# Convolved blocks turned by VectorE and DRAM instead of TensorE, with a longer weight rotation at the pooled blocks

## The chip, the core and the metric

The kernel runs on one core of a Trainium2 chip. The metric is the device time of one execution in microseconds (us). A core has five engines that run their own instruction streams and wait for each other by semaphores: TensorE (PE in the profile; its weight loads are PEld), VectorE (DVE), ScalarE (ACT), GpSimd (POOL) and SyncE (SP), which here only issues transfers. ScalarE and GpSimd issue transfers too. The profile shows issuing in the queue rows (SPq, ACTq). On-chip memory has 128 partitions; a tile is a rectangle of partitions and bytes in it.

## The reference

One layer of a diffusion backbone in float32: 512 latent tokens and 256 context tokens of width 1024. After a modulated RMSNorm, one projection (1024 columns in, 4640 out) feeds three groups of heads. What matters here is the beginning of that:

```
p = u @ w_in                                # u: normalised, modulated tokens
z, xbc, dt, pool, q, k, v = split(p)        # widths 1024, 1536, 32, 512, 512, 512, 512
xbc = silu(dwconv(xbc, conv_w, conv_b))     # 3 taps along the tokens, per channel
xs, B, C = split(xbc)                       # 1024, 256, 256 channels
pooled = [mean over w neighbours - pool  for w in (2, 4, 8, 16)]   # 128 channels each
y = pooled @ w_pool * pool_scale
```

xs, B and C go into a state space scan in both directions (SSD), k and v with q into a neighbourhood attention. The modulation vectors are `silu(c) @ ada_w + ada_b`, with a matrix of 1024 x 6144; two of its six parts are needed only at the second half of the layer. Behind all this come the output projection, another normalisation, and a feed-forward part that picks 16 of 16,384 experts for each of 8 heads (PEER).

## The kernel before, in words

**Three matmuls for one.** Float32 products are made from split operands: `h` is the rounded high part, `l` the remainder, and `mm3` adds h·h, h·l and l·h (L220 to L222, and L460 to L466 where latent and context tokens share the weights). For that, each weight block is loaded to a tile `wraw` by SP (L241), ScalarE makes `wh` from it (L210), VectorE makes `wl` (L213).

**The weight stream.** `Stream` (L224 to L250) keeps a list of raw tiles and a list of split pairs and goes around both in turn: load number i takes raw tile i modulo the length of the list. Through the stage of interest there are three raw tiles ("G") and two split pairs, and `ws.keep(3, 2)` ahead of it sets the counters to 0. `extend` adds tiles to a list, `keep` cuts the lists and resets the counters.

**The stage around the change** (54 to 217 us of the span), on TensorE:

1. Twelve blocks of 128 channels of xbc, the loop `for cb in range(12)` (L664). Blocks 0 to 7 are xs, 8 and 9 B, 10 and 11 C. `projT` (L522) loads a weight block and makes the block transposed: channels on partitions, 512 latent tokens in one PSUM bank and, for blocks under 10, 256 context tokens in another. ScalarE copies both into `xp` (L669, L672), VectorE makes the three taps in `c1` (L675 to L677), ScalarE the silu (L683, for C blocks L679). Since xs and B are needed with tokens on partitions too, TensorE turns each of the ten blocks in six transposes of 128x128 (L687 four, L693 two) into PSUM; VectorE copies four back (L688) and ScalarE two (L694), into `xsn` (six tiles of 128 tokens by 1024 channels) or `Bn`. The tiles of this loop, `xp`, `c1`, `sT` and others, are in the pool `tmpC` on the right side of memory, closed at L698.
2. Four pooled blocks, b = 3 to 0 (L737 on). Each has two `projT`: PL (the pooled channels) and K (keys). GpSimd sums the windows (`pool_sums`, L711), VectorE subtracts (`pool_diff`), TensorE multiplies by w_pool (`pool_out`). The pool `plp` of this stage, with `pl`, `pa`, `pb`, lies on the right side as well, where `tmpC` was.
3. Decays and V0: `decays` (L756) and four loads of `projC`. Then `plp` is closed, and the SSD stage begins; it reads `xsn` first at L902.

Beside this, the modulation sums run on VectorE: `ada_sum(bank, k)` (L551) multiplies two pieces of ada_w, 128 x 1024 each, by a scalar per partition and adds them up in `adac`. SP loads each piece into one of the input tiles that are free by then, `xin` = three parts of kT, qT0, qT1, vc; from the tenth step on into the last three of them in turn (L558). One step of this generator `ada` is taken in blocks cb >= 3 and twice per pooled block; the sums keep their program order on VectorE.

**What sets the order.** The streams of each engine are put in order by the scheduler of the language from the code's dependences; those marked `keep_in_program_order` keep the order of the code. Tiles of a closed pool give their memory to the pool opened next; an instruction that writes such memory waits until the former readers and writers are done.

Of the kernel before, what the change touches and what calls it, by code (L numbers as in the profile page):

```python
# [7 lines left out]
F32 = mybir.dt.float32  # L8
# [4 lines left out]
AF = mybir.ActivationFunctionType  # L13
ALU = mybir.AluOpType
# [143 lines left out]
def build(tc, A, out, dbg=None):  # L158
    nc = tc.nc
    V, S, G, PE = nc.vector, nc.scalar, nc.gpsimd, nc.tensor  # L160
    dbg = dbg or {}

    def dump(name, ap):
        if name in dbg:
            nc.sync.dma_start(dbg[name], ap)
# [53 lines left out]
    def mm3(ps, ah, al, bh, bl, start, stop):  # L219
        PE.matmul(ps, ah, bh, start=start, stop=False)  # L220
        PE.matmul(ps, ah, bl, start=False, stop=False)  # L221
        PE.matmul(ps, al, bh, start=False, stop=stop)  # L222
# [29 lines left out]
    def kpc(src):  # L252
        return src.rearrange("(k p) c -> p k c", p=P)
# [13 lines left out]
    ident = cst[:, C_ID:C_ID + P]  # L267
# [40 lines left out]
    ws = Stream()  # L308
# [11 lines left out]
    xsn = si.tile([P, NT, D], F32, name="xsn")  # L320
    Bn = si.tile([P, NT, 256], F32, name="Bn")
# [13 lines left out]
    psT = gps.ps("psT", bufs=2)  # L335
# [22 lines left out]
    xin = [kf[:, t * D:(t + 1) * D] for t in range(3)] + [q0f, q1f, vf]  # L358
# [98 lines left out]
    def mm_xc(px, pc, h, l, k, part=""):  # L457
        s, e = k == 0, k == KB - 1
        if part != "l":
            PE.matmul(px, h[:, k, :], uh[:, k, :], start=s, stop=False)  # L460
            PE.matmul(pc, h[:, k, :], uch[:, k, :], start=s, stop=False)
            PE.matmul(px, h[:, k, :], ul[:, k, :], start=False, stop=False)  # L462
            PE.matmul(pc, h[:, k, :], ucl[:, k, :], start=False, stop=False)
        if part != "h":
            PE.matmul(px, l[:, k, :], uh[:, k, :], start=False, stop=e)  # L465
            PE.matmul(pc, l[:, k, :], uch[:, k, :], start=False, stop=e)  # L466
# [80 lines left out]
    ad1 = adp.sb("ad1")  # L547

    adac = {}

    def ada_sum(bank, k):  # L551

        if k == 0:
            adac[bank] = ad1.tile([P, 2048], F32, name="adac", bufs=2)
        part = adac[bank]
        n = (bank - 1) * KB + k
        for jj in range(2):
            w = xin[(2 * n + jj) % NT] if n < 10 else xin[3 + (2 * n + jj) % 3]  # L558
            nc.sync.dma_start(w, A["ada_w"][k * P:(k + 1) * P, (bank - 1) * 2048 + jj * 1024:(bank - 1) * 2048 + (jj + 1) * 1024])
            dst, ck = part[:, jj * 1024:(jj + 1) * 1024], cc[:, k, 0:1]  # L560
            if k:
                tc.keep_in_program_order(V.scalar_tensor_tensor(dst, w, ck, dst, ALU.mult, ALU.add))
            else:
                tc.keep_in_program_order(V.tensor_scalar(dst, w, ck, None, ALU.mult))
# [40 lines left out]
    tp = cvp.sb("tmpC", bufs=2, side="right")  # L605
# [58 lines left out]
    for cb in range(12):  # L664
        if cb in (1, 4, 5):
            next(dtp, None)
        px, pc = early[cb] if cb < 3 else projT(A["w_in"][:, XBC0 + cb * P:XBC0 + (cb + 1) * P], cb < 10)
        xp = xps[cb % 2]
        S.activation(xp[:, 1:513], px, AF.Copy)  # L669
        n = SEQ  # L670
        if cb < 10:
            S.activation(xp[:, 515:771], pc[:, :CTX], AF.Copy)  # L672
            n = 770
        c1 = tp.tile([P, 770], F32, name="c1")[:, :n]
        V.tensor_scalar(c1, xp[:, 1:n + 1], convw[:, 12 + cb:13 + cb], convb[:, cb:cb + 1], ALU.mult, ALU.add)  # L675
        V.scalar_tensor_tensor(c1, xp[:, 0:n], convw[:, cb:cb + 1], c1, ALU.mult, ALU.add)
        V.scalar_tensor_tensor(c1, xp[:, 2:n + 2], convw[:, 24 + cb:25 + cb], c1, ALU.mult, ALU.add)  # L677
        if cb >= 10:
            S.activation(CT[:, cb - 10, :], c1, AF.Silu)  # L679
            next(ada, None)  # L680
            continue
        sT = tp.tile([P, 770], F32, name="sT") if cb < 8 else BT[:, cb - 8, :]
        S.activation(sT, c1, AF.Silu)  # L683
        dst = xsn[:, :, cb * P:(cb + 1) * P] if cb < 8 else Bn[:, :, (cb - 8) * P:(cb - 7) * P]
        pt = psT.tile([P, 4, P], F32, name="pt")
        for j in range(4):
            PE.transpose(pt[:, j, :], sT[:, j * P:(j + 1) * P], ident)  # L687
        V.tensor_copy(dst[:, 0:4, :], pt)  # L688
        if cb >= 3:
            next(ada, None)  # L690
        pt = psT.tile([P, 4, P], F32, name="pt")
        for j in range(2):
            PE.transpose(pt[:, j, :], sT[:, 514 + j * P:514 + (j + 1) * P], ident)  # L693
# [12 lines left out]
    nc.scalar.dma_start(pcnt, A["pcnt"].rearrange("p (w t) -> p w t", w=4))
    nc.scalar.dma_start(pw, A["pool_w"].rearrange("p (w t) -> p w t", w=4))
    LP = SEQ + 16
    pls = {}

    def pool_sums(b, px):  # L711

        pl = pl2.tile([P, LP], F32, name="pl")
        G.memset(pl[:, 0:8], 0.0)
        G.memset(pl[:, 520:528], 0.0)
        S.activation(pl[:, 8:520], px, AF.Copy)
        cur, nxt = pl2.tile([P, LP], F32, name="pa"), pl2.tile([P, LP], F32, name="pb")
        G.tensor_tensor(cur[:, 1:528], pl[:, 0:527], pl[:, 1:528], ALU.add)
        for w in WINDOWS[1:b + 1]:
            d, lo = w // 4, w // 2  # L720
            G.tensor_tensor(nxt[:, lo:LP - lo], cur[:, lo - d:LP - lo - d], cur[:, lo + d:LP - lo + d], ALU.add)
            cur, nxt = nxt, cur
        G.tensor_tensor(cur[:, 8:16], cur[:, 8:16], pcnt[:, b, 0:8], ALU.mult)
        G.tensor_tensor(cur[:, 512:520], cur[:, 512:520], pcnt[:, b, 8:16], ALU.mult)
        pls[b] = (pl, cur, nxt)

    def pool_diff(b):
        pl, cur, nxt = pls[b]
        tc.keep_in_program_order(V.scalar_tensor_tensor(nxt[:, 8:520], cur[:, 8:520], 1.0 / WINDOWS[b], pl[:, 8:520], ALU.mult, ALU.subtract))

    def pool_out(b):
        _, dst, src = pls.pop(b)
        pp = psG.tile([P, 512], F32, name="acc")
        tc.keep_in_program_order(PE.matmul(pp, pw[:, b, :], src[:, 8:520], start=True, stop=True))
        S.activation(dst[:, 8:520], pp, AF.Copy, scale=pscale[:, b:b + 1])
        nc.scalar.dma_start(mix_d[8 + b], dst[:, 8:520])
    for b in (3, 2, 1, 0):  # L737
        px, _ = projT(A["w_in"][:, PL0 + b * P:PL0 + (b + 1) * P], False)
        if b < 3:
            pool_diff(b + 1)  # L740
        next(ada, None)
        pool_sums(b, px)
        px, pc = projT(A["w_in"][:, K0 + b * P:K0 + (b + 1) * P])
        if b < 3:
            pool_out(b + 1)
        if b == 0:
            pool_diff(0)
        next(ada, None)
        S.activation(kT[:, b, :SEQ], px, AF.Copy)
        S.activation(kT[:, b, SEQ:], pc[:, :CTX], AF.Copy, scale=-1.0)  # L750
# [35 lines left out]
    psT = psp.ps("psT1", bufs=1)  # L786
# [269 lines left out]
    for c in range(4):  # L1056
        b = U0 + UP * c
# [11 lines left out]
    for c in range(4):  # L1069
        b = O1 + OP * c  # L1070
# [129 lines left out]
    pT, tT = {}, {}  # L1200
# [154 lines left out]
    def out_w(kk, half):  # L1355
        return wspl(wload(w_out(kk, half)), 2)
# [36 lines left out]
    for kk in (6, 7):  # L1393
        w = ispls["w", kk]
# [5 lines left out]
    for i, kk in enumerate((4, 5, 0, 1, 2)):  # L1400
        w = out_w(kk, 1) if i else ispls["h", kk]
# [859 lines left out]
```

## Time and profile before

| | us |
|---|---|
| median of 3 runs | 1715.47 |
| lowest, highest | 1713.44, 1716.55 |
| profiled execution, its own time | 1716.2 |
| span of its instructions | 1714.3 |
| TensorE busy | 1691.8 (99%) |
| VectorE busy | 1412.5 (82%) |
| ScalarE busy | 834.2 (49%) |
| GpSimd busy | 387.1 (23%) |

The granted clock of TensorE is 0.998 on average. The span begins with the first instruction and ends with the last; the rest of the execution's time is around it. A timeline row gives the start in us from the span's beginning, the length in us (of several instructions in a row, where it ends with xN, from first start to last end), engine, line, operation, tiles out and in, shapes, and in brackets the idle time of the engine ahead of it with what ended it. A row of groups gives busy time and mean ns of one behind the bar. A row of a named source gives shortest, median and longest duration in ns and the starts of the first and last.

### The profile page before, as it was taken

Reading aid. Unit: us, or ns where it says so; the run is one execution under the profiler, and the core shown is the slowest. Engines: PE = TensorE matmul, PEld = TensorE weight load, DVE = VectorE, ACT = ScalarE, POOL = GpSimd, SP = SyncE. Lnnn points to the kernel's source line nnn. Section 1 sums busy time; section 2 is a strip of 40 time slices with the busy share of each in tenths; the row PEclk is TensorE's granted clock in tenths of the full one; section 3 lists DMA queues with packets and bytes.
Section 4 is the critical chain, followed back from the end, with each engine's and each line's share of the span. In section 5 each row is a group of like instructions: output and inputs, shape, how many; then the busy total and the mean of one; then the engine's idle time right before and its main releaser. Section 6 shows DMA issues by size and latency. Waiting matters only on the chain.

```text
span 1714.3 us, 26441 instructions
## 1 busy us (share of the span) xinstructions
PE 1691.8 (99%) x9516; PEld 1467.6 (86%) x9516; DVE 1412.5 (82%) x2678; ACT 834.2 (49%) x1497; POOL 387.1 (23%) x307
## 2 busy tenths in 40 slices
PE   9999999999999999999999999999999999999997
PEld 7888777776789889999999998888888888888886
DVE  6689479977645699889989997998898889889886
ACT  5443355565444333556766764444444444444444
POOL 0003134012426444032212112212211211212200
PEclk9999999999999999999999999999999999999999
DMA  9457556497736334587989999999999999999972
GB/s 374 130 158 225 161 197 182 148 299 218 222 116 193 106 119 137 170 325 271 340 334 348 348 327 357 385 414 357 392 369 381 367 414 384 380 368 381 388 270 107
DMA packets 204244, 478.33 MB, mean 279 GB/s; under 512 B 15544, under 2 KB 122136, under 8 KB 186160
## 3 DMA queue, kind: packets, MB, share of 16 engines
q1 hardware_dynamic: 154464, 271.04, 45.9%
q0 software_dynamic: 21136, 144.83, 22.1%
q10 hardware_dynamic: 28512, 60.76, 9.6%
q8 instruction: 75, 1.23, 0.3%
q14 instruction: 57, 0.47, 0.1%
HBM read 420.79 MB, written 57.88 MB: 279 GB/s over the span
## 4 chain that ended last, share of the span: by engine, by line
PE 78%; DVE 9%; DMA 6%; ACT 4%; issue 2%; ACTq 1%; POOL 0%; SPq 0%; DVEq 0%; POOLq 0%
PE pv L221 10%; PE pv L222 10%; PE pv L220 10%; PE pu L222 7%; PE pu L220 7%; PE pu L221 7%; PE acc L220 5%; PE acc L222 5%; PE acc L221 5%; DMA act_d<-act 4%; DVE wl L213 2%; PE acc L460 1%; PE acc L465 1%; PE acc L462 1%; ACT wh L210 1%
## 5 line engine op out<-in xcount | busy, mean ns | idle before, releaser
L210 ACT ACTIVATE wh<-wraw 128x1024 fp32r<-128x1024 f32 x328 | 342.1, 1054 | 216.9 <-PE acc L221 75.7
L213 DVE TENSOR_TENSOR wl<-wraw,wh 128x1024 fp32r<-128x1024 f32 x295 | 361.9, 1238 | 84.5 <-ACT wh L210 83.7
L220 PE MATMUL pu<-u2h,wh 128*128 128x368 f32 x1008 | 337.1, 334 | 1.5 <-ACT act L1555 1.4
L222 PE MATMUL pu<-u2h,wl 128*128 128x368 f32 x1008 | 332.5, 330 | 0.6 <-DVE wl L213 0.6
L221 PE MATMUL pu<-u2l,wh 128*128 128x368 f32 x1008 | 332.0, 329 | 0.0
L222 PE MATMUL pv<-wh,wwl 128*128 128x512 f32 x768 | 299.6, 390 | 0.0
L221 PE MATMUL pv<-wl,wwh 128*128 128x512 f32 x768 | 299.5, 390 | 0.0
L220 PE MATMUL pv<-wh,wwh 128*128 128x512 f32 x768 | 299.3, 390 | 0.1
L1834 POOL DMA_INDIRECT row<-in_peer_uv,idxG x128 | 158.7, 1240 | 617.9 <-DVE accG L1848 578.1
L220 PEld LDWEIGHTS pu<-u2h,wh 128*128 128x128 f32 x1008 | 189.8, 188 | 3.4 <-ACT act L1555 2.0
L222 PEld LDWEIGHTS pu<-u2h,wl 128*128 128x128 f32 x1008 | 189.6, 188 | 1.9 <-DVE wl L213 1.8
L221 PEld LDWEIGHTS pu<-u2l,wh 128*128 128x128 f32 x1008 | 189.9, 188 | 1.4
L210 ACT ACTIVATE wwh<-gd 128x384 fp32r<-128x384 f32 x124 | 65.1, 525 | 242.5 <-DVE gd L2079 224.4
L222 PEld LDWEIGHTS pv<-wh,wwl 128*128 128x128 f32 x768 | 144.2, 188 | 30.3 <-DVE wwl L213 0.3
L220 PEld LDWEIGHTS pv<-wh,wwh 128*128 128x128 f32 x768 | 144.3, 188 | 29.2 <-ACT wwh L210 0.5
L221 PEld LDWEIGHTS pv<-wl,wwh 128*128 128x128 f32 x768 | 144.2, 188 | 29.0
L1848 DVE SCALAR_TENSOR_TENSOR accG<-row,wG,accG 128x1024 f32<-128x1024 f32 x127 | 162.4, 1279 | 1.6
L1839 DVE CUSTOM_DVE_ANT_0 row<-row,u2G 128x1024 f32<-128x1024 f32 x128 | 154.8, 1218 | 0.0
L1922 ACT ACTIVATE stg<-gdps 128x512 f32<-128x512 f32 x96 | 101.0, 1163 | 19.2 <-ACT act L1555 15.3
L213 POOL TENSOR_TENSOR wl<-wraw,wh 128x1024 fp32r<-128x1024 f32 x33 | 79.1, 2401 | 101.6 <-ACT wh L210 70.9
L1555 ACT ACTIVATE act<-pu 128x368 f32<-128x368 f32 x90 | 42.6, 473 | 105.6 <-PE pu L222 58.8
L213 DVE TENSOR_TENSOR wwl<-gd,wwh 128x384 fp32r<-128x384 f32 x124 | 68.9, 556 | 21.9 <-ACT wwh L210 21.9
(482 smaller groups left out, 3004.7 us busy)
## 6 DMA issues: line engine op xcount, KB each, us to landing
wraw<-in_peer_ut SPq DMA_DIRECT2D x128, 512.0 KB
wraw<-in_peer_uv SPq DMA_DIRECT2D x128, 512.0 KB
gd<-gd_d SPq DMA_DIRECT2D x15, 1536.0 KB
gd_d<-stg ACTq DMA_DIRECT2D x11, 2048.0 KB
wraw<-in_w_in SPq DMA_DIRECT2D x40, 512.0 KB
acl<-act_d SPq DMA_DIRECT2D x92, 184.0 KB
act_d<-act ACTq DMA_DIRECT2D x90, 184.0 KB
cs<-cs_d SPq DMA_DIRECT2D x32, 256.0 KB
```

The source lines that it names most:

```text
L210: S.activation(hi, full, AF.Copy)
L213: (eng or V).tensor_tensor(lo, full, hi.bitcast(F32), ALU.subtract)
L220: PE.matmul(ps, ah, bh, start=start, stop=False)
L221: PE.matmul(ps, ah, bl, start=False, stop=False)
L222: PE.matmul(ps, al, bh, start=False, stop=stop)
L460: PE.matmul(px, h[:, k, :], uh[:, k, :], start=s, stop=False)
L462: PE.matmul(px, h[:, k, :], ul[:, k, :], start=False, stop=False)
L1555: S.activation(act, pu[:, :TU], AF.Gelu)
L1834: G.indirect_dma_start(out=rows[k], out_offset=None, in_=A["peer_uv"], in_offset=bass.IndirectOffsetOnAxis(ap=idxG[:, k:k + 1], axis=0))
L1839: V.tensor_tensor_reduce(row[:, 0:D], row[:, 0:D], u2G, 1.0, 0.0, ALU.mult, ALU.add, actG[:, k:k + 1])
L1848: V.scalar_tensor_tensor(accG, row[:, D:2 * D], wG[:, k:k + 1], accG, ALU.mult, ALU.add)
L1922: S.activation(stg[:, :, t0:t0 + 4].rearrange("p a t -> p t a"), ps, AF.Copy, scale=1.0 if full else 1.0 / GSCALE)
```

## The change

- In blocks 0 to 9 the six TensorE transposes with their two copies go. VectorE's `transpose`, which turns each 32x32 square in place, writes the block into a new tile `tT` (128 x 768, three of them, in `tmpC`): 512 columns, then 256. Four transfers issued by GpSimd, one for each 32 partitions, put the squares in their places in a DRAM array `xc_d` (768 tokens by 1280 channels). Each writes 768 pieces of 128 bytes.
- `rows_back(b)`, behind each `pool_sums(b)`, has GpSimd load the rows back: six transfers of 512 KB for `xsn`, one of 768 KB for `Bn`. GpSimd's operations of the pooled stage now keep their program order.
- Pool `plp` gets two tiles `xl0`, `xl1`, and from the tenth step on the modulation pieces go around five tiles (`xlate`) instead of three.
- At the beginning of the pooled stage two raw weight tiles ("P", in `plp`) are added to the stream's list, which has five then. At its end `ws.keep(3, 2)` takes them off and sets the counters to 0.

```diff
+    xc_d = tc.dram_tile([NTOK, 10 * P], F32, name="xc_d")
...
     adac = {}
+    xlate = xin[3:]
...
-            w = xin[(2 * n + jj) % NT] if n < 10 else xin[3 + (2 * n + jj) % 3]
+            w = xin[(2 * n + jj) % NT] if n < 10 else xlate[(2 * n + jj) % len(xlate)]
...
         S.activation(sT, c1, AF.Silu)
-        dst = xsn[:, :, cb * P:(cb + 1) * P] if cb < 8 else Bn[:, :, (cb - 8) * P:(cb - 7) * P]
-        pt = psT.tile([P, 4, P], F32, name="pt")
-        for j in range(4):
-            PE.transpose(pt[:, j, :], sT[:, j * P:(j + 1) * P], ident)
-        V.tensor_copy(dst[:, 0:4, :], pt)
+        tT = tp.tile([P, NTOK], F32, name="tT", bufs=3)
+        V.transpose(tT[:, 0:SEQ], sT[:, 0:SEQ])
+        V.transpose(tT[:, SEQ:], sT[:, 514:770])
+        for q in range(4):
+            c0 = cb * P + 32 * q
+            nc.gpsimd.dma_start(xc_d[:, c0:c0 + 32].rearrange("(n p) j -> p n j", p=32), tT[32 * q:32 * q + 32, :].rearrange("p (n j) -> p n j", j=32))
         if cb >= 3:
             next(ada, None)
-        pt = psT.tile([P, 4, P], F32, name="pt")
-        for j in range(2):
-            PE.transpose(pt[:, j, :], sT[:, 514 + j * P:514 + (j + 1) * P], ident)
-        S.activation(dst[:, 4:6, :], pt[:, 0:2, :], AF.Copy)
+    rowt = {3: (5,), 2: (4, "B"), 1: (3, 2), 0: (1, 0)}
+
+    def rows_back(b):
+        for t in rowt[b]:
+            if t == "B":
+                ins = nc.gpsimd.dma_start(Bn, xc_d[:, D:].rearrange("(t p) c -> p t c", p=P))
+            else:
+                ins = nc.gpsimd.dma_start(xsn[:, t, :], xc_d[t * P:(t + 1) * P, 0:D])
+            tc.keep_in_program_order(ins)
     cvp.close()
...
     pw = pl1.tile([P, 4, P], F32, name="pw")
+    xlate += [pl1.tile([P, D], F32, name=f"xl{i}") for i in range(2)]
+    ws.extend(plp, "P", 2, 0, "right")
...
         pool_sums(b, px)
+        rows_back(b)
         px, pc = projT(A["w_in"][:, K0 + b * P:K0 + (b + 1) * P])
...
     plp.close()
+    ws.keep(3, 2)
     adp.close()
```

More of the change, by code (lines that the diff above doesn't have):

```diff
@@ L683, in build @@
         S.activation(sT, c1, AF.Silu)
-        dst = xsn[:, :, cb * P:(cb + 1) * P] if cb < 8 else Bn[:, :, (cb - 8) * P:(cb - 7) * P]
-        pt = psT.tile([P, 4, P], F32, name="pt")
-        for j in range(4):
-            PE.transpose(pt[:, j, :], sT[:, j * P:(j + 1) * P], ident)
-        V.tensor_copy(dst[:, 0:4, :], pt)
+        tT = tp.tile([P, NTOK], F32, name="tT", bufs=3)
[4 more added lines that the diff above has]
+            nc.gpsimd.dma_start(xc_d[:, c0:c0 + 32].rearrange("(n p) j -> p n j", p=32), tT[32 * q:32 * q + 32, :].rearrange("p (n j) -> p n j", j=32))
         if cb >= 3:
             next(ada, None)
-        pt = psT.tile([P, 4, P], F32, name="pt")
-        for j in range(2):
-            PE.transpose(pt[:, j, :], sT[:, 514 + j * P:514 + (j + 1) * P], ident)
-        S.activation(dst[:, 4:6, :], pt[:, 0:2, :], AF.Copy)
-    dump("xsn", xsn)
-    dump("Bn", Bn)
-    dump("CT", CT)
+    dump("CT", CT)
+    rowt = {3: (5,), 2: (4, "B"), 1: (3, 2), 0: (1, 0)}
[6 more added lines that the diff above has]
+            tc.keep_in_program_order(ins)
     cvp.close()
@@ L713, in pool_sums @@
         pl = pl2.tile([P, LP], F32, name="pl")
-        G.memset(pl[:, 0:8], 0.0)
-        G.memset(pl[:, 520:528], 0.0)
+        tc.keep_in_program_order(G.memset(pl[:, 0:8], 0.0))
+        tc.keep_in_program_order(G.memset(pl[:, 520:528], 0.0))
         S.activation(pl[:, 8:520], px, AF.Copy)
         cur, nxt = pl2.tile([P, LP], F32, name="pa"), pl2.tile([P, LP], F32, name="pb")
-        G.tensor_tensor(cur[:, 1:528], pl[:, 0:527], pl[:, 1:528], ALU.add)
+        tc.keep_in_program_order(G.tensor_tensor(cur[:, 1:528], pl[:, 0:527], pl[:, 1:528], ALU.add))
         for w in WINDOWS[1:b + 1]:
             d, lo = w // 4, w // 2
-            G.tensor_tensor(nxt[:, lo:LP - lo], cur[:, lo - d:LP - lo - d], cur[:, lo + d:LP - lo + d], ALU.add)
+            tc.keep_in_program_order(G.tensor_tensor(nxt[:, lo:LP - lo], cur[:, lo - d:LP - lo - d], cur[:, lo + d:LP - lo + d], ALU.add))
             cur, nxt = nxt, cur
-        G.tensor_tensor(cur[:, 8:16], cur[:, 8:16], pcnt[:, b, 0:8], ALU.mult)
-        G.tensor_tensor(cur[:, 512:520], cur[:, 512:520], pcnt[:, b, 8:16], ALU.mult)
+        tc.keep_in_program_order(G.tensor_tensor(cur[:, 8:16], cur[:, 8:16], pcnt[:, b, 0:8], ALU.mult))
+        tc.keep_in_program_order(G.tensor_tensor(cur[:, 512:520], cur[:, 512:520], pcnt[:, b, 8:16], ALU.mult))
         pls[b] = (pl, cur, nxt)
```

## The prediction

> **What bounds the kernel now.** I read the page's busy time, then the table by stretches of the span, then the timelines of single engines around the convolved blocks.
>
> ```profile
> PE 1691.8 (99%) x9516; PEld 1467.6 (86%) x9516; DVE 1412.5 (82%) x2678; ACT 834.2 (49%) x1497; POOL 387.1 (23%) x307
> 50.00:100.00 50.00, 49.77 (x297) 42.30 (x297) 34.00 (x55) 21.16 (x37) 0.00 (x0) 1.00 0.41 124
> 100.00:150.00 50.00, 49.96 (x274) 41.36 (x273) 45.22 (x57) 22.62 (x35) 1.61 (x7) 1.00 0.61 181
> 150.00:200.00 50.00, 50.00 (x258) 41.72 (x257) 31.23 (x26) 11.90 (x18) 20.18 (x20) 1.00 0.64 210
> ```
>
> The columns of the stretches are TensorE (PE), its weight loads, VectorE (DVE), ScalarE (ACT), GpSimd (POOL), granted clock, DMA share, GB/s. Every stretch that the change touches has TensorE busy to the last tenth at full clock. So a microsecond taken off TensorE there is a microsecond gained, and one in which it stands still is lost. VectorE is near its limit in the second stretch; GpSimd is free until 147 us. The question is whether any new wait reaches TensorE.
>
> **The gain: 60 transposes.** The transposes stand between matmuls of the next block; what they cost is read from the starts of the matmuls around them (start, length):
>
> ```profile
> 66.65 0.39 PE L629 MATMUL acc<-ul,whl 128*64 128x512 f32 x1
> 66.88 0.66 PE L687 MATMUL pt<-cst,sT 128*128 128x128 f32 x4
> 67.37 0.38 PE L693 MATMUL pt<-cst,sT 128*128 128x128 f32 x2
> 67.51 0.36 PE L629 MATMUL acc<-ucl,whl 128*64 128x256 f32 x1
> 72.51 0.40 PE L460 MATMUL acc<-uh,wh 128*128 128x512 f32 x1
> 72.97 0.66 PE L687 MATMUL pt<-cst,sT 128*128 128x128 f32 x4
> 73.46 0.38 PE L693 MATMUL pt<-cst,sT 128*128 128x128 f32 x2
> 73.60 0.36 PE L461 MATMUL acc<-uch,wh 128*128 128x256 f32 x1
> 73.80 0.40 PE L462 MATMUL acc<-ul,wh 128*128 128x512 f32 x1
> 74.03 0.28 PE L463 MATMUL acc<-ucl,wh 128*128 128x256 f32 x1
> ```
>
> An undisturbed 512-column matmul is followed after 0.23 us (73.80 to 74.03). With the six transposes between it is 0.86 us (66.65 to 67.51), or 1.09 (72.51 to 73.60) where they also wait for the silu. That is 0.63 to 0.86 us a block; ten blocks make 6.3 to 8.6 us. I take 7, between the two, as the wait is not in every block.
>
> **What pays for it elsewhere.** VectorE loses one copy a block and gets two 32x32-block transposes (128x512 and 128x256). Another place of the kernel already runs the first; GpSimd's plain transfers are also there in small number:
>
> ```profile
> L688 DVE COPY xsn<-pt 128x512 f32<-128x512 f32 x8 | 5.5, 687 | 5.3 <-PE pt L687 5.3
> L1213 DVE STREAM_TRANSPOSE tT<-pr x10: 692/706/712, 394.7 to 437.0; 128x512 f32<-128x512 f32 x10
> L1641 POOL DMA_DIRECT2D si_d<-ixS x1: 599/599/599, 727.2 to 727.2; - x1
> L1451 POOL DMA_DIRECT2D xs_d<-xn x1: 737/737/737, 511.5 to 511.5; - x1
> ```
>
> So +0.02 us for the large one, and an estimated 0.4 (a little over half of 0.706) for the small one: +0.4 us a block, off the path while VectorE has idle time (34.0 busy of 50), on it near the end. ScalarE loses its 0.38 us copy. GpSimd gets 40 issues. The si_d write, 128 pieces of 64 bytes, took 0.60 us; the xs_d one, 16 rows of 4 KB, took 0.74. Mine has 768 pieces of 128 bytes. Below: 0.6 us each, 24 us in all on an idle engine. Above: the price grows with the pieces, 768/128 x 0.6 = 3.6 us. I take 0.75, as a few pieces more or less hardly moved the two rows. The seven loads back (3.8 MB, 11 us at the 349 GB/s which the first 50 us of this profile moved) lie between the pooled sums:
>
> ```profile
> 0.00:50.00 50.00, 47.16 (x379) 37.37 (x380) 29.64 (x79) 25.60 (x50) 0.41 (x5) 1.00 0.94 349
> 194.47 0.20 POOL L724 TENSOR_TENSOR pa<-pa,pcnt 128x8 f32<-128x8 f32 x1
> 217.90 0.68 DVE L902 TENSOR_TENSOR xd<-xsn,enB 128x512 f32<-128x512 f32 x1
> ```
>
> Between the last sum and the first reader are 23 us for two 0.5 MB loads: nothing, at 1.5 us each plus a latency of 3.35 (below). If that cover went, xd at L902 would be late.
>
> **The new wait.** The two added raw weight tiles join the rotation at once, and block loads 0 to 8 (cb 3 to 11) have used places 0, 1, 2. The next load, for the first pooled block (PL3), has number 9, and 9 modulo 5 is 4: an added tile. It lies in memory that the convolution's pool gives back. In the built program, bytes 145,664 to 149,760 of a partition lie over a tT tile that GpSimd's last writes read, and xl0 (175,104 to 179,200) over c1, the convolution's output of block 11. Where SP now stands, the change:
>
> ```order
> L561 DMA kT_120<-in_ada_w 128x1024 x2
> L561 DMA qT0_121<-in_ada_w 128x1024
> L561 DMA xl0_1461<-in_ada_w 128x1024
> L561 DMA qT1_122<-in_ada_w 128x1024
> L561 DMA vc_123<-in_ada_w 128x1024
> L561 DMA xl1_1462<-in_ada_w 128x1024
> L241 DMA wraw_1472<-in_w_in 128x8x128
> ```
>
> and the kernel before, where wraw_1432 is block 11's load and wraw_1493 PL3's:
>
> ```order
> L241 DMA wraw_1432<-in_w_in 128x8x128
> L241 DMA wraw_1493<-in_w_in 128x8x128
> L559 DMA kT_119<-in_ada_w 128x1024 x2
> L241 DMA wraw_1552<-in_w_in 128x8x128
> L559 DMA kT_119<-in_ada_w 128x1024
> ```
>
> PL3's weights were the load right after block 11's; now they (wraw_1472) stand behind xl0, which waits for ScalarE's last silu, and behind vc, which waits for VectorE's sums. ScalarE shows the same in the change (CT from c1_1435 is block 11's silu, wh_1474 PL3's split, acc_1409 block 11's sums):
>
> ```order
> L671 ACTIVATE xp1_709<-acc_1409 128x512
> L681 ACTIVATE CT_133<-c1_1435 128x512
> L714 DMA pcnt_1469<-in_pcnt 128x64
> L715 DMA pw_1460<-in_pool_w 128x512
> L210 ACTIVATE wh_1474<-wraw_1472 128x1024
> L210 ACTIVATE wh_1534<-wraw_1532 128x1024
> ```
>
> Before, PL3's split stood eight rows ahead of that silu. TensorE's own order is unchanged here, PL3 directly after block 11, so it stands still until PL3's weights are there.
>
> **How long.** The tail of block 11 before:
>
> ```profile
> 140.15 0.39 PE L222 MATMUL acc<-uh,wl 128*128 128x512 f32 x1
> 140.38 0.39 PE L220 MATMUL acc<-uh,wh 128*128 128x512 f32 x1
> ...
> 134.12 1.06 ACT L210 ACTIVATE wh<-wraw 128x1024 fp32r<-128x1024 f32 x1 [4.28 <-issue]
> 146.81 0.63 ACT L679 ACTIVATE CT<-c 128x512 f32<-128x512 f32 x1
> ...
> 144.11 1.22 DVE L213 TENSOR_TENSOR wl<-wraw,wh 128x1024 fp32r<-128x1024 f32 x1
> 146.02 0.75 DVE L677 SCALAR_TENSOR_TENSOR c<-xp,colv,c 128x512 f32<-128x512 f32 x1
> 147.35 0.75 DVE L564 TENSOR_SCALAR adac<-vc,cc 128x1024 f32<-128x1024 f32 x1
> ...
> 147.46 0.33 SPq L559 DMA_DIRECT2D qT<-in_ada_w  x1
> 148.13 0.33 SPq L559 DMA_DIRECT2D vc<-in_ada_w  x1
> ```
>
> TensorE ends block 11 and begins PL3 at 140.4; VectorE ends the convolution at 146.77, 6.4 us later. That lag harmed nothing, because PL3's split was made at 134.1. Now it counts, step by step, on the clock of the profile before:
> - Block 11 ends on TensorE at 140.4 - 7 = 133.4.
> - Convolution ends at 133.4 + 6.4 + 0.8 = 140.6 (0.8: the transposes of the two last blocks before it, 0.4 each). Lower bound: the two splits (1.2 us each) of PL3 and K3 that leave this stretch give 2.4 back. Upper: up to 4 us more, if VectorE keeps its old pace instead of TensorE's new one.
> - Silu 0.63: 141.2, and xl0 goes out. The two VectorE starts of the next sum end 1.3 us behind the convolution, as now, so vc goes out at 142.0, xl1 at 142.4, wraw_1472 at 142.8.
> - Landing, from rows of the same queue:
>
> ```profile
> 160.89 0.33 SPq L559 DMA_DIRECT2D qT<-in_ada_w  x1
> 164.24 2.03 DVE L562 SCALAR_TENSOR_TENSOR adac<-qT,cc,adac 128x1024 f32<-128x1024 f32 x1 [2.12 <-DMA qT<-in_ada_w]
> 154.43 2.23 DVE L562 SCALAR_TENSOR_TENSOR adac<-vc,cc,adac 128x1024 f32<-128x1024 f32 x1 [1.13 <-DMA vc<-in_ada_w]
> ```
>
> One load alone took 3.35 us from issue to its reader. The vc issued at 148.13 behind two others took 6.3, which is 3.35 plus two times the 1.5 that 512 KB take at 349 GB/s. With four ahead of it that went out from 141.3, wraw_1472 lands at 141.3 + 3.35 + 4 x 1.5 = 150.6. Lower bound 142.8 + 3.35 = 146.2, the others costing nothing.
> - Split on ScalarE, 1.06: TensorE starts PL3 at 151.7. Its third matmul needs wl, 1.23 later, when two matmuls (0.46) have run: 0.8 more.
>
> Sum: 151.7 - 140.4 + 0.8 = **12 us lost, net**, the 7 us of transposes already inside; TensorE stands still some 19 us. Nothing later gives it back: in the 50 us after 150 TensorE has no idle time to fill, and its order there is the same. The rest of the longer rotation and xl0, xl1 fetch ahead for an engine that did not wait in that stretch. The reset of the rotation at the stage's end I cost at nothing: TensorE, VectorE and GpSimd keep their order behind it, and only a few loads and splits near 500 us trade places.
>
> The profiled execution took 1716.2 us (span 1714.3), 0.7 above the median of 1715.47. 1716.2 + 12 = 1728.2, by the median's standard 1727.5; I say 1728.
>
> Bounds of this case: convolution 2.4 early, landing at its least, gain 8.6: 12 - 2.4 - 4.4 - 1.6 = +4 (1720). Convolution 4 late: +16 (1732).
>
> **Rivals.**
> *GpSimd's writes are slow, and the load waits for them.* PL3's load must also await the last writes that read the tile under it. The last tT is ready some 7 us before the convolution's end (133.5), four issues and a landing at 0.75 each end at 133.5 + 3 + 3.35 = 139.9, before 142.8. From about 1.5 us an issue they decide, and from 2 us (a block's four then take the 8 us that TensorE needs for a block) a backlog grows from the first block at 60.5: at 2.5 us the last is issued at 160.5, lands at 163.9, the load after it at 167.2; with split and wl 1.9 later that is +29 (1745). At 3.6: 60.5 + 144, then 3.35 + 3.35 + 1.9, +73 (1789). For it: no row here has 768 pieces. Against: 128 pieces cost less than 16 large rows.
>
> There is a second way to it: GpSimd's issue waits until a VectorE instruction beside it ends. If each of 40 waited one out (1.02 to 1.27 us here) it would cost 1.6 to 1.9, just at the point where it decides: +12 to +16. The Trainium skill, "SBUF — State Buffer", section "A bandwidth-pool intuition that's wrong (but worth ruling out)", says a transfer issued by GpSimd takes about 620 ns alone and about 3100 beside a VectorE copy, as its descriptors wait for a shared port. By that figure alone, an estimate, 40 x 3.1 = 124 us would run to 184 and the time be some 1769. The trace's one to three such issues, at 511 and 727 us, do not show which holds.
>
> *The load is not late: the other side.* If wraw_1472 went out before 129, that is 133.4 less 3.35 less 1.06, TensorE would run on and only the 7 us would be left: 1709. It breaks even when PL3 starts at 140.4, a load landing by 138.5. For it: the loads for K3, PL2 and K2 stand ahead and are in place. Against: the queue's order, and the 6.4 us of lag.
>
> *No change:* lag and landing at their least with a convolution that catches up with TensorE: 134.0 (xp 0.58), three instructions 2.04, silu 0.63, four issues 1.6, 3.35, 1.06 and 0.8 make a stop of 10 us against 7 to 8.6: still +1.4 to +3, at the edge of what can be told from no change, about 0.2% or 3.4 us.
>
> **How the numbers follow.** The stop at PL3 by SP's queue 0.70, nearly all of it slower by over 0.2%; writes that decide 0.22 (half of these below 1745, and 0.08 of it for VectorE holding GpSimd's issues up); load not late 0.05; no change 0.03. Range 1719 to 1745: it leaves out the upper half of the slow writes (0.11) and the load in time (0.05). Faster 0.04, within 0.2% 0.04, slower 0.92. I predict 1728.
>
> **What would show it.** Right: one idle stretch of TensorE of 15 to 22 us before the first L220 of PL3 (acc from wh), released by ScalarE's wh, that by the landing of wraw; SP's load issued after xl0, 2 us behind block 11's silu; 60 L687/L693 rows gone, and block pitch shorter by 0.6 to 0.9. Wrong: GpSimd's xc_d issues above 1.5 us each; the stop released by a DMA on xc_d; no stop at all; a second stop at L902 for xsn.

## The result, and the profile after

The changed kernel takes 1731.37 us in the median of six runs (1726.96 to 1733.39), the kernel before beside it 1715.61 (six runs, 1713.44 to 1718.40). The ratio is 1.0087, 95% interval 1.0069 to 1.0105: slower by 15 us, where 1728 (1719 to 1745) was forecast. The profiled execution of the changed kernel took 1729.79 us, 13.6 more than that of the kernel before; there +12 was forecast.

Busy time of the engines on the page after, then the table by stretches of the span (same columns as before):

```profile
PE 1687.7 (98%) x9456; PEld 1463.8 (85%) x9456; DVE 1414.4 (82%) x2688; ACT 833.0 (48%) x1489; POOL 414.5 (24%) x354
50.00:100.00 50.00, 50.00 (x290) 42.57 (x289) 41.11 (x75) 26.27 (x39) 16.87 (x23) 1.00 0.57 165
100.00:150.00 50.00, 34.40 (x181) 28.88 (x179) 37.40 (x46) 13.54 (x21) 12.98 (x20) 0.87 0.82 247
150.00:200.00 50.00, 46.60 (x231) 37.82 (x232) 27.98 (x26) 11.20 (x16) 15.73 (x26) 0.93 0.73 230
```

TensorE has 60 instructions fewer, and busy time lower by 4.1 us. But from 100 to 150 us it is busy for 34.4 us where it had 49.96, and the clock granted in the last two stretches is 0.87 and 0.93 where it was 1.00. TensorE's timeline shows the place:

```profile
134.01 0.39 PE L222 MATMUL acc<-uh,wl 128*128 128x512 f32 x1
153.37 0.80 PE L220 MATMUL acc<-uh,wh 128*128 128x512 f32 x1 [18.96 <-ACT wh L210]
...
154.62 0.80 PE L222 MATMUL acc<-uh,wl 128*128 128x512 f32 x1
...
156.07 0.63 PE L222 MATMUL acc<-uh,wl 128*128 128x512 f32 x1
156.50 0.63 PE L220 MATMUL acc<-uh,wh 128*128 128x512 f32 x1
...
161.04 1.07 PE L575 MATMUL acc<-adac,cst 128*32 128x512 f32 x8
```

134.01 is the last matmul of block 11, 153.37 the first of PL3, 161.04 the first after PL3 (the modulation sums over partitions, L573 before). What led there, from the timelines of VectorE, ScalarE and SP after, in this order of engines:

```profile
139.79 0.75 DVE L679 SCALAR_TENSOR_TENSOR c<-xp,colv,c 128x512 f32<-128x512 f32 x1
140.57 0.63 ACT L681 ACTIVATE CT<-c 128x512 f32<-128x512 f32 x1 [5.48 <-DVE c L679]
152.26 2.00 ACT L210 ACTIVATE wh<-wraw 128x1024 fp32r<-128x1024 f32 x2 [11.05 <-DMA wraw<-in_w_in]
141.23 0.33 SPq L561 DMA_DIRECT2D xl<-in_ada_w  x1
...
142.13 0.38 SPq L561 DMA_DIRECT2D vc<-in_ada_w  x1
142.56 0.74 SPq L561 DMA_DIRECT2D xl<-in_ada_w  x1
143.65 14.84 SPq L241 DMA_DIRECT2D wraw<-in_w_in  x4
```

This is the chain of the prediction: convolution's end, silu, xl0, the next modulation pieces, then PL3's weights; ScalarE waits 11 us for these and TensorE 19.

How much of the slowing comes from here is read from the starts of that sum over partitions, the first and the last of its 16 matmuls. The rows of its line before and after (durations in ns, then starts of the first and last):

```profile
L573 PE MATMUL acc<-adac,cst x16: 592/605/617, 145.9 to 200.9; 128*32 128x512 f32 x16
```
```profile
L575 PE MATMUL acc<-adac,cst x16: 592/605/617, 161.0 to 216.0; 128*32 128x512 f32 x16
```

The changed kernel is 15.1 us behind at the first and as much at the last: the whole pooled stage keeps the distance. For every kernel below, **first** and **last** stand for these two starts against the kernel before. Further on the changed kernel is 18.7 behind at the start of the neighbourhood attention's output and 13.7 at the span's end.

### The profile page after: what moved, and what is told of

Same layout as the page of the kernel before. It is cut to its first block, busy times and chain, and to the rows that moved or that the text cites. A ratio compares the mean times of both kernels' runs of the same rounds, so it can differ in the third digit from the quotient of the medians.

```text
span 1728.0 us, 26422 instructions
## 1 busy us (share of the span) xinstructions
PE 1687.7 (98%) x9456; PEld 1463.8 (85%) x9456; DVE 1414.4 (82%) x2688; ACT 833.0 (48%) x1489; POOL 414.5 (24%) x354
## 4 chain that ended last, share of the span: by engine, by line
PE 84%; DVE 8%; DMA 3%; ACT 2%; issue 2%; POOL 0%; ACTq 0%; SPq 0%; DVEq 0%; POOLq 0%
PE pv L222 10%; PE pv L221 10%; PE pv L220 10%; PE pu L220 9%; PE pu L222 9%; PE pu L221 9%; PE acc L220 5%; PE acc L222 5%; PE acc L221 5%; DVE wl L213 2%; PE acc L461 1%; PE acc L466 1%; PE acc L463 1%; DMA xc_d<-tT 1%; PE gdps L1930 1%
## 5 line engine op out<-in xcount | busy, mean ns | idle before, releaser
L213 DVE TENSOR_TENSOR wl<-wraw,wh 128x1024 fp32r<-128x1024 f32 x295 | 357.6, 1223 | 95.5 <-ACT wh L210 94.0
L1858 DVE SCALAR_TENSOR_TENSOR accG<-row,wG,accG 128x1024 f32<-128x1024 f32 x127 | 162.5, 1280 | 1.6
```

What stands on the lines that cost most here:

```text
L213: (eng or V).tensor_tensor(lo, full, hi.bitcast(F32), ALU.subtract)
L1858: V.scalar_tensor_tensor(accG, row[:, D:2 * D], wG[:, k:k + 1], accG, ALU.mult, ALU.add)
```

## Experiments

| kernel | time, us | beside it, before | ratio, 95% interval | first | last |
|---|---|---|---|---|---|
| changed kernel | 1731.37 | 1715.61 | 1.0087 [1.0069, 1.0105] | +15.1 | +15.1 |
| e2: turn alone | 1720.18 | 1714.64 | 1.0029 [1.0017, 1.0042] | -6.6 | +6.1 |
| e3: tiles alone | 1715.89 | 1714.64 | 1.0006 [0.9993, 1.0018] | +1.5 | +1.5 |
| e5: without xl0, xl1 | 1726.77 | 1715.28 | 1.0079 [1.0060, 1.0098] | +12.4 | +12.4 |
| e1: old tile first | 1716.99 | 1714.57 | 1.0027 [1.0012, 1.0042] | -6.6 | +4.0 |
| e4: TensorE kept busy | 1727.26 | 1714.64 | 1.0073 [1.0056, 1.0089] | +13.1 | +13.1 |
| e7: no reset | 1727.34 | 1714.64 | 1.0083 [1.0063, 1.0103] | +13.9 | +13.9 |
| e6: without P tiles | 1714.26 | 1714.57 | 1.0006 [0.9994, 1.0018] | -6.8 | -0.8 |
| e8: e6, rows back late | 1714.14 | 1714.57 | 1.0007 [0.9994, 1.0020] | -6.6 | 0.0 |
| e9: e2, rows back late | 1714.81 | 1714.57 | 1.0008 [0.9998, 1.0018] | -6.6 | -1.0 |
| e11: e6, tT in another pool | 1712.60 | 1715.28 | 0.9986 [0.9973, 0.9999] | -6.2 | -1.6 |
| e16: e11, subtraction ahead | 1705.96 | 1715.28 | 0.9955 [0.9938, 0.9972] | -5.8 | -6.6 |

The theory under test: PL3's load comes late because its place in the rotation is a P tile and its place in SP's queue is behind xl0. Rivals: it is late through GpSimd's writes, or the turning itself costs what TensorE saves.

### e2, the turn alone

From the changed kernel:

```diff
-    xlate += [pl1.tile([P, D], F32, name=f"xl{i}") for i in range(2)]
-    ws.extend(plp, "P", 2, 0, "right")
...
-    ws.keep(3, 2)
```

> The changed kernel without the two added raw weight tiles and without xl0, xl1 (three raw tiles and three late modulation tiles, as before; no reset of the counters); the blocks are still turned by VectorE and GpSimd's transfers. PL3's load now stands before the convolution's last block on SP again. Theory (the stop comes from the place of PL3's load): no stop at PL3, TensorE begins PL3 right behind block 11, 6 us earlier than before (134.2 against 140.4, as the changed kernel's block 11 ended), and the time is 1715.6 - 6 = 1709.6. Rival (the writes through DRAM are what is late, since the chain of waits of the changed kernel went through a 5.3 us landing of xc_d): TensorE still waits 5 us or more at PL3 or later for xsn, 1715 to 1725.

No stop at PL3, as the theory has it, and the gain is whole at that point: -6.6 us. But then 12.7 us are lost between the first and the last sum. Two stops of TensorE carry it. The first is at the pooled product (pool_out, L740 here). The second is at a weight's low part (wl) that stands behind a late modulation piece; GpSimd's loads back of two row tiles go out just ahead of that piece (rows of TensorE, GpSimd, SP, VectorE, TensorE):

```profile
167.81 2.04 PE L740 MATMUL acc<-pa,pw 128*128 128x512 f32 x2 [4.28 <-issue]
...
183.59 1.10 POOL L702 DMA_DIRECT2D xsn<-xc_d  x2
184.81 0.33 SPq L561 DMA_DIRECT2D qT<-in_ada_w  x1
192.85 1.28 DVE L564 SCALAR_TENSOR_TENSOR adac<-qT,cc,adac 128x1024 f32<-128x1024 f32 x1 [3.38 <-DMA qT<-in_ada_w]
194.05 3.23 DVE L213 TENSOR_TENSOR wl<-wraw,wh 128x1024 fp32r<-128x1024 f32 x2
196.19 0.50 PE L466 MATMUL acc<-uh,wl 128*128 128x512 f32 x1 [3.89 <-DVE wl L213]
```

The piece is used 8.0 us after its issue, where one alone took 3.35 before. On VectorE the sum stands ahead of wl, whose high part was ready at 186.0, so wl begins only at 194.05, and TensorE waits for it. (An earlier piece, vc, was used 8.2 us after its issue, at 178.31, and no stop of TensorE followed.) So the forecast of 1709 for "the load in time" falls. What the pooled stage lost is taken up by e6 to e16.

### e3, the tiles alone

To the kernel before are added the two xl tiles, `ws.extend(plp, "P", 2, 0, "right")` and `ws.keep(3, 2)`; the transposes stay on TensorE.

> The kernel before with the two raw weight tiles, xl0, xl1 and the reset of the counters, but with TensorE's transposes as before. Without the tT tiles the memory under PL3's new tile is free from block 2 on, and SP issues that load there, well ahead of block 11. Theory (the stop needs both: the tile in the rotation and the tT tiles under it): no stop, within 4 us of 1715.6. Rival (the longer rotation alone puts PL3's load late): a stop at PL3 of 12 to 19 us, 1728 to 1735.

No stop of TensorE at PL3 and no change that can be told. With the old memory layout PL3's load goes out early although it goes to a P tile. The stop needs both parts of the change: the longer rotation (e2 has none and no stop), and the turn. Whether it is the memory of the tT tiles in the turn, or its other effects on SP's order, was not tried apart.

### e5, the raw tiles without xl0 and xl1

```diff
-    xlate += [pl1.tile([P, D], F32, name=f"xl{i}") for i in range(2)]
```

> The changed kernel without xl0 and xl1, with the two raw weight tiles (the rotation and its reset as in the change). PL3's tile now lies over other memory, that of the dt part and of a tT of blocks 1, 4 and 7, which is free by 125; but SP still issues its load behind two pieces that wait for VectorE's sums of block 11. Theory (the place in SP's queue is enough): TensorE stops at PL3 for 16 to 19 us, as in the changed kernel less the two xl loads ahead (up to 2 us): 1727 to 1731. Rival (the stop comes from the memory under the new tile or from xl0's wait for the silu): 1716 or less.

The stop is there without the xl tiles. TensorE and SP of e5:

```profile
150.02 0.80 PE L220 MATMUL acc<-uh,wh 128*128 128x512 f32 x1 [16.78 <-ACT wh L210]
140.75 0.33 SPq L561 DMA_DIRECT2D vc<-in_ada_w  x1
141.43 13.72 SPq L241 DMA_DIRECT2D wraw<-in_w_in  x4
```

PL3's load still stands behind vc, which waits for VectorE's sums. It goes out 2.2 us earlier than in the changed kernel and lands 7.5 us later instead of 8.6. So the xl tiles make about 2.7 us of the +15.1 (first: +12.4), and vc alone is enough for the rest.

### e1, PL3's load into an old tile

```diff
     ws.extend(plp, "P", 2, 0, "right")
+    ws.i = 0
```

> The changed kernel with one line more: the counter of raw tiles is set to 0 when the two tiles are added, so that PL3, K3 and PL2 take the three old tiles and K2 the first new one. SP then issues PL3's load right behind block 11's. Theory (the stop at PL3 is the tile's place in the rotation): no stop at PL3, first modulation row of TensorE (L575) 6.6 us earlier than before, as in the run without added tiles; what is left of that at the SSD stage shows whether five modulation tiles and five raw tiles carry the pooled stage: 1709 if they do. Rival (the pooled stage cannot be fed any faster with the rows coming back beside it): the 6.6 us are lost again before the SSD stage, as in the run without added tiles, 1716 to 1721.

The counter at 0 makes PL3 and the next two loads take old tiles; the P tiles take the fourth and fifth load. The stop at PL3 is gone (first -6.6), as the theory wants. It comes back at the fourth block, K2, whose load is now the first for a P tile:

```profile
163.66 0.79 PE L461 MATMUL acc<-uh,wh 128*128 128x512 f32 x1 [8.63 <-ACT wh L210]
```

So the place of the load, not what the load carries, makes the stop: in both kernels the block that has the first P tile waits. Three blocks later it is less than half as long. The time is 1717.0: the 1709 that was expected if the 6.6 us survived is missed.

### e4, TensorE kept busy

Between block 11 and PL3, 78 matmuls go to a PSUM tile that nobody reads (work beyond the reference):

```diff
+    warm = psT.tile([P, 4, P], F32, name="pt").rearrange("p a b -> p (a b)")
+    for i in range(78):
+        tc.keep_in_program_order(PE.matmul(warm, uh[:, i % KB, 0:P], uh[:, i % KB, :], start=True, stop=True))
```

> The changed kernel with 78 more matmuls of 128x512 on TensorE between block 11 and PL3, into a PSUM tile that nobody reads (17.8 us at 0.228 us each, so TensorE idles 1 us there instead of 19). In the changed kernel the granted clock was 0.50 through the stop, and PL3's first seven matmuls followed each other after 0.43 to 0.66 us instead of 0.23, which made PL3 7.7 us long against 5.5. Theory (the idle time itself lets the clock down, and its return is paid after it): PL3 starts at the same 153.4 but runs at full pace, 2.2 us less: 1729.2. Rival (the slow first matmuls are late operands, or the clock falls for another reason): no difference, 1731.4.

In the changed kernel the granted clock falls and comes back around the stop (its stretches of a microsecond each; clock is the number third from the end):

```profile
136.00:137.00 1.00, 0.00 (x0) 0.00 (x0) 1.00 (x2) 0.00 (x0) 0.89 (x2) 0.82 0.75 152
137.00:138.00 1.00, 0.00 (x0) 0.00 (x0) 1.00 (x2) 0.00 (x0) 0.00 (x0) 0.50 1.03 256
...
156.00:157.00 1.00, 1.00 (x4) 0.73 (x3) 1.00 (x2) 0.00 (x0) 0.00 (x0) 0.50 0.79 220
157.00:158.00 1.00, 1.00 (x6) 0.82 (x5) 1.00 (x1) 0.00 (x0) 0.00 (x0) 0.94 0.97 292
```

With TensorE kept busy PL3 runs at its usual pace of 0.23 us a matmul, but for the wait for wl:

```profile
133.82 17.84 PE L747 MATMUL pt<-uh 128*128 128x512 f32 x78
152.55 0.50 PE L220 MATMUL acc<-uh,wh 128*128 128x512 f32 x1 [0.89 <-ACT wh L210]
...
159.02 1.06 PE L575 MATMUL acc<-adac,cst 128*32 128x512 f32 x8
```

From PL3's start to the first sum it takes 159.02 - 152.55 = 6.47 us, in the changed kernel 161.04 - 153.37 = 7.67. The slow clock costs 1.2 us. (From the kernel before it is 1.3: PL3 took 145.91 - 140.38 = 5.53 there, and 0.8 of the difference is the wait for wl.) The other 0.8 between +13.1 and +15.1 is there at PL3's start already (152.55 against 153.37) and so is not the clock behind the stop. Of the 2.2 us that were expected to be the clock's, 0.8 is the wait for wl. In time e4 and the changed kernel cannot be told apart: the intervals overlap.

### e7, no reset of the rotation

```diff
-    ws.keep(3, 2)
+    ws.raw = ws.raw[:3]
```

> The changed kernel, but at the end of the pooled stage the two added raw tiles are taken off the list without setting the counters of the rotation to 0. In the changed kernel's profile the attention stage, 150 us later, lost a further 3.4 us (its first L1248 group came 18.7 us later than before, while the stage between had kept +15.1), at a wait of ScalarE for an nb transfer that took 6.1 us instead of 3.7 beside a weight load issued 10 us earlier than before. Theory A (the reset gives that load another tile, and so another time): the group comes 15.1 us later than before, and the time is 1731.4 - 3.4 = 1728.0. Theory B (it is the timing that the stop left behind, or chance): unchanged, 18.7 us and 1731.4.

In the profiles the reset costs something. The stretch from 217 to 500 us, of the changed kernel and then of e7:

```profile
217.00:500.00 283.00, 274.92 (x1457) 204.65 (x1456) 211.27 (x382) 150.38 (x340) 73.56 (x58) 0.99 0.64 198
```
```profile
217.00:500.00 283.00, 277.51 (x1476) 207.35 (x1476) 212.28 (x382) 151.05 (x341) 74.38 (x58) 1.00 0.64 199
```

TensorE is busy 2.6 us less with the reset. One place is seen in the changed kernel: ScalarE's split stands behind the wait for a bias tile (nb) whose transfer shares its time with a weight load, and TensorE waits for the softmax behind it:

```profile
383.86 1.06 ACT L210 ACTIVATE wh<-wraw 128x1024 fp32r<-128x1024 f32 x1 [2.51 <-DMA nb<-in_nabias]
385.55 0.85 PE L1207 MATMUL pt<-cst,pr 128*128 128x128 f32 x4 [2.68 <-ACT pT L1217]
```

In the profile theory A holds: the attention's output begins 13.4 us later than before in e7, whose sums are 13.9 behind, and 18.7 in the changed kernel, whose sums are 15.1 behind. Between the first and the last transposes of the softmax (L1207) the changed kernel lost 3.4 us against the kernel before, e7 -0.2. Over all kernels the two groups touch: those with the reset (also e1, e3, e4, e5) lost 1.0 to 4.0 us, those without it (also e2, e6, e8, e9, e11, e16) between -0.2 and +0.9. In time it is not to be told: 1.0083 against 1.0087.

### e6, without the P tiles

```diff
-    ws.extend(plp, "P", 2, 0, "right")
...
-    ws.keep(3, 2)
```

> The changed kernel with xl0 and xl1 but with the three old raw tiles only and no reset. In the run without any added tiles TensorE was 6.6 us ahead at the first L575 and 6.1 us behind at the last: modulation pieces landed 8 us after their issue (vc issued at 170.1 beside xsn and Bn loads of GpSimd issued at 168.9 and 169.5), and VectorE's weight split stood behind their sums. Theory (with five tiles the pieces are loaded one sum earlier, which hides 8 us): the 6.6 us survive to the SSD stage, 1709 to 1711. Rival (raw tiles are short too, or the pieces come late all the same): 1716 to 1720.

The modulation pieces have their two more tiles, and the 12.7 us of e2 shrink to 6.0. All of it is one stop, at the product, and the slow clock behind that. TensorE, ScalarE, GpSimd and VectorE of e6:

```profile
167.58 2.04 PE L741 MATMUL acc<-pa,pw 128*128 128x512 f32 x2 [4.28 <-issue]
148.83 1.06 ACT L210 ACTIVATE wh<-wraw 128x1024 fp32r<-128x1024 f32 x1 [5.50 <-PE acc L464]
154.64 1.06 ACT L210 ACTIVATE wh<-wraw 128x1024 fp32r<-128x1024 f32 x1 [3.99 <-PE acc L221]
155.61 1.07 ACT L723 ACTIVATE pl<-acc 128x512 f32<-128x512 f32 x2
156.34 1.55 POOL L725 TENSOR_TENSOR pa<-pl 128x527 f32<-128x527 f32 x1 [12.29 <-ACT pl L723]
162.98 1.06 ACT L210 ACTIVATE wh<-wraw 128x1024 fp32r<-128x1024 f32 x1 [6.31 <-PE acc L464]
164.07 1.95 DVE L213 TENSOR_TENSOR wl<-wraw,wh 128x1024 fp32r<-128x1024 f32 x1 [7.11 <-ACT wh L210]
165.94 1.53 DVE L736 SCALAR_TENSOR_TENSOR pa<-pb,pl 128x512 f32<-128x512 f32 x1
```

PL3 was done at 139, yet ScalarE copies its result (pl, L723) at 155.6, behind two splits that wait for TensorE. GpSimd's window sum starts 12 us late for that. The subtraction (L736) then stands on VectorE behind K1's wl, which waits until TensorE frees a split pair at 163; TensorE has meanwhile come to the pooled product, which waits for the subtraction. Why pl stands so late in ScalarE's order is tried in e11: the pooled tiles lie where tT was, so that they must wait for GpSimd's last writes out of tT. On the chip that wait is long over by 155 (GpSimd clears the edges of pl at 143.4); what is late is the place that the scheduler gave the copy.

### e8 and e9, the rows back later

`rows_back` goes out of the loop, behind all pooled blocks; e8 is e6 with this edit, e9 is e2 with it.

```diff
-        rows_back(b)
...
+    for b in (3, 2, 1, 0):
+        rows_back(b)
```

> As the run with xl0 and xl1 only, and GpSimd's seven loads back are all moved behind the last pooled sums (3.8 MB between some 189 us and the first reader at 211). Theory (the rows coming back slow the modulation pieces): pieces land in 3.5 to 6 us in the pooled stage, the 6.6 us survive, 1709; a wait for xsn at the SSD stage's first product of up to 3 us may appear, 1712. Rival (they do not): the same as with the rows between the sums, or worse by that wait.

> As the run without any added tiles (1720.2), with GpSimd's seven loads back moved behind the last pooled sums. It tells whether the rows coming back are what cost that run its 12.7 us between the first and the last L575. Theory (they are, through the modulation pieces' landing): the largest part, 8 us or so, comes back, 1710 to 1714. Rival (it is the order of VectorE, split before difference, and the three tiles): 1718 to 1721.

In e8 little changes: the stop at L741 stays (3.67 us), the last sum comes 0.8 us later than in e6. In e9 the edit brings back 7.1 us of the 12.7 (last -1.0 instead of +6.1). So without the xl tiles the loads back bring about the second stop of e2. With the xl tiles VectorE still waits longer for a piece beside the loads back (3.10 us in e6, at most 0.50 in e8 at that place), but TensorE does not stop for it. The stop at the product is another matter and is in all four of these kernels (4.28 us in e2 and e6, 3.67 in e8 and e9).

### e11, tT in another pool

```diff
-        tT = tp.tile([P, NTOK], F32, name="tT", bufs=3)
+        tT = ad1.tile([P, NTOK], F32, name="tT", bufs=3)
```

on e6: `ad1` closes at the end of the whole stage, so the pooled tiles no longer lie over tT.

> The run with xl0 and xl1 only, with the tT tiles in the pool that closes at the end of the stage, and nothing else. It tells the place of tT from the order on VectorE. Theory: pl goes out at some 144 and GpSimd's sums end at 151, but VectorE's difference is still behind the split for K1 (164.1 to 165.3), so TensorE waits 2.6 us at L741 instead of 4.3: about 3 of the 6 us come back, 1711. Rival (the place of tT has nothing to do with the late copy): pl stays at 155.6, 1714.

The copy moves ahead of the splits, and the stop at the product shrinks to 2.65 us, as the theory has it. The last sum comes only 0.8 us earlier than in e6, though, where about 3 us were expected (ScalarE and TensorE of e11):

```profile
144.78 0.60 ACT L723 ACTIVATE pl<-acc 128x512 f32<-128x512 f32 x1 [0.90 <-ACT CT L681]
166.51 2.07 PE L741 MATMUL acc<-pa,pw 128*128 128x512 f32 x2 [2.65 <-DVE pa L736]
```

### e16, the subtraction ahead of the next block's wl

On e11, `pool_diff(b + 1)` and the next step of the modulation sums go behind K's `projT` in the code, and on VectorE what K's `projT` issues, its wl among it, comes only after the subtraction of two blocks before:

```diff
+        with tc.issue_after(diffs[b + 2].ins) if b < 2 else ExitStack():
+            px, pc = projT(A["w_in"][:, K0 + b * P:K0 + (b + 1) * P])
```

> As the run with xl0 and xl1 only (1714.3, no change), with two things set right. There the first pooled copy (pl of PL3) waited on ScalarE until 155.6 although PL3 was done at 139, since its memory counts as held by the tT tiles and the scheduler put it behind two weight splits; the sums of GpSimd came 7 us late, VectorE's difference stood behind the split for K1, and TensorE waited 4.3 us at the pooled product L741 and ran slowly for 2 us after it: 6 us, the whole gain. Now the tT tiles are in a pool that closes at the end of the stage, so that the pooled tiles wait for no xc_d transfer, and the difference is issued ahead of K1's split on VectorE. Theory (that one stop ate the gain): pl at some 144, no stop at L741, TensorE stays 6.6 us ahead at the SSD stage: 1708. Rival (the stage has no slack, another wait takes its place): stop elsewhere between 155 and 205, 1711 to 1715.

This beats both kernels: 0.9955 of the kernel before, interval 0.9938 to 0.9972, that is 5 to 11 us. VectorE of e16, and then its stretch from 150 us:

```profile
157.00 1.56 DVE L736 SCALAR_TENSOR_TENSOR pa<-pb,pl 128x512 f32<-128x512 f32 x1
...
164.87 1.21 DVE L213 TENSOR_TENSOR wl<-wraw,wh 128x1024 fp32r<-128x1024 f32 x1
```
```profile
150.00:200.00 50.00, 50.00 (x255) 39.97 (x254) 29.42 (x26) 15.50 (x29) 23.02 (x30) 1.00 0.83 289
```

The subtraction is done at 158.6 instead of 167.5 (e6), and TensorE is busy in all of this stretch at full clock. The 6.6 us reach the last sum whole. (The first stands at -5.8 as four matmuls of K3 come ahead of that sum in this kernel.)

## Why the prediction was right, and where it was off

**Direction, place and mechanism** were as forecast, for the reason given: the stop before PL3, released by wh and that by wraw, with SP's load behind xl0 and vc. e1 bears out the rotation, e3 that it needs the turn beside it, and e5 the place in SP's queue. No wait for xsn appeared: its first reader starts at 233.0, 15.1 us later than before (217.9), like the sums ahead of it. The steps, each on the clock of its own profile:

| step | forecast | measured |
|---|---|---|
| block 11's end on TensorE | 133.4 | 134.24 |
| end of the convolution | 140.6 | 140.54 |
| wraw of PL3 issued | 142.8 | 143.65 |
| its landing, seen by its reader | 150.6 | 152.3 |
| PL3 starts | 151.7 | 153.37 |
| extra for wl | 0.8 | 0.8 |
| slow clock behind the stop | not in the sum | 1.2 to 1.3 |
| kept to the last sum | +12 | +15.1 |

- *The gain* was 6.1 us (140.38 to 134.24 on TensorE), in e2 6.6, where 7 was taken from 6.3 to 8.6. The lower bound was the better value: six transposes cost the 0.63 us of a block without a wait.
- *The tail of the convolution* came out within 0.1 us, and that is luck: block 11 ended 0.84 later than forecast, and the lag behind it was 6.3 us (134.24 to 140.54) where 6.4 + 0.8 = 7.2 was summed. The split that stood in the lag before (144.11) had gone from it.
- *The issue* of wraw came 0.85 later than forecast, mostly since the last xl held the queue for 0.74 instead of 0.33 and wraw followed 0.35 behind it; *its landing* 8.6 us after the issue instead of 7.8. These two mis-sized terms make 1.7 us.
- *The clock* is the term that was left out. The first matmuls of PL3 follow each other after 0.43 us (156.07 to 156.50) and more instead of 0.23. The clock falls 2.2 us after TensorE's last matmul has ended (134.40 to about 136.6) and is back 3.7 us after the first new one (157.1). The Trainium skill, "TensorE: Matmul & The Clock Gate", section "Part 1: The HAM clock gate", gives half rate after an idle window of about 3.4 us and full rate after a busy one, the windows running freely. The trace agrees with the half rate and roughly with the return; the fall came sooner than that window. Where a stop of TensorE of some microseconds is forecast, this belongs in the sum.
- *Gives nothing back later*: right through to the last sum (+15.1 and +15.1). Behind it the attention stage took 3.6 us more and the rest gave 5 back, neither of them forecast; that the span ends at +13.7, so near to +12, is luck. The claim that longer rotation and xl tiles "fetch ahead for an engine that did not wait in that stretch" was right of the kernel before. It was wrong of the kernel whose load is in time: there the xl tiles are worth 6.7 us (e2's 12.7 against e6's 6.0).
- *The reset at nothing*: not borne out by the profiles, which show 3.6 us between the changed kernel and e7 in the attention stage, though this is too small to be told in time. "TensorE, VectorE and GpSimd keep their order" was no ground for it: the few loads that trade places were enough to make a split late.

**GpSimd's writes.** The forecasts of 0.75 us an issue and of 0.4 for the small transpose were right. The rows of the xc_d array and the tT tile in the changed kernel:

```profile
L691 POOL DMA_DIRECT2D xc_d<-tT x40: 715/717/1170, 64.0 to 136.2; - x40
L688 DVE STREAM_TRANSPOSE tT<-sT x8: 401/403/434, 63.0 to 117.5; 128x256 f32<-128x256 f32 x8
DMA to landing us min/median/max: 2.4/4.9/5.9
...
142.27 0.10 POOL L722 MEMSET pl<- 128x8 f32 x1 [5.38 <-DMA xc_d<-tT]
```

No issue was held up to the 1.6 us at which this rival decided, although VectorE was busy 41 of 50 us beside them; the longest took 1.17. The Trainium skill's 3100 ns for a GpSimd transfer beside a VectorE copy ("SBUF — State Buffer", "A bandwidth-pool intuition that's wrong (but worth ruling out)") does not appear in these 40. What was undersized is the landing: 3.35 was taken, 4.9 is the median. The last writes were in by 142.27, 1.4 us before wraw's issue at 143.65, where 139.9 against 142.8 was forecast. So the rival lost by 1.4 us instead of 2.9, and in a kernel with the P load placed a little earlier the writes would decide.

**The load in time, 1709,** had the mechanism right and the price wrong. With the load in time e2 takes 1720 and e6 1714. "The 7 us would be left" holds only at PL3: the pooled stage has a stop of its own then. The kernel before had room for 7 us at this place (rows of VectorE and TensorE before):

```profile
158.99 0.68 DVE L729 SCALAR_TENSOR_TENSOR pa<-pb,pl 128x512 f32<-128x512 f32 x1
169.87 1.02 PE L734 MATMUL acc<-pa,pw 128*128 128x512 f32 x2
```

There pl was copied at 148.36 and the subtraction was done 10.2 us ahead of the product. In e6 pl is copied at 155.6 and the subtraction done at 167.5, 7.8 us later than before. So the stop is not the price of an earlier TensorE alone: the change's own tiles and the new order on VectorE took the room away. Only when the copy of pl, the pooled sum and the subtraction are in time too (e16) does the gain reach the end: 1706.

**What stays open.** In the last part of the kernel, the feed-forward, the shift changes by -7.0 us (e16) to +1.4 (e2) from profile to profile (the changed kernel makes up 5 us there); what sets this was not tried. Of the 13.1 us by which e16's profiled span is shorter than the one before, 7.0 come there. By the medians e16 is 9.3 us faster; the runs account for 6.6 of these.

## What to carry to other kernels

When an engine that never idles is given less to do, the copy, sum or load that it meets next is due earlier: look one stage further for what can now be late, and for what the change itself makes late there, and price it. Adding tiles to a rotation changes which load gets which memory: find the first load that lands in a new tile, what that memory held last, and what stands ahead of it in the issuing queue. A tile read by a slow transfer, in a pool whose memory the next stage takes, holds up that stage's order and not only its first writer.

## What the runs showed of the hardware

- A GpSimd transfer of 768 pieces of 128 bytes costs 0.72 us to issue, as much as one of 16 rows of 4 KB (0.74); it lands after 4.9 us in the median. Why so late for 96 KB was not tried.
- A stop of 19 us costs 1.2 to 1.3 us more than its length, as matmuls run at half clock for 3.7 us after it; stops of 4.28 us (e2) and 2.65 us (e11) are long enough for the clock to fall, too: behind e11's it is 0.50 from 167 to 169 us. The stretch behind the one in e2:

```profile
168.00:170.00 2.00, 2.00 (x3) 0.95 (x4) 2.00 (x2) 0.11 (x1) 2.00 (x3) 0.50 0.68 214
```
